# Feed-forward products of a two-layer trunk: seven half-size products for eight, with h through DRAM

## The chip, the cores and the metric

The kernel runs on one core of a Trainium2 chip. The metric is the time of one execution on the device, in microseconds (us). Before the change three runs took 2847.48, 2851.25 and 2854.4 us; the median is 2851.25.

## What is computed

Two layers, each a token-mixing sublayer and a gated feed-forward, in float32, for 1024 tokens of width 1024:

```python
x = layer_norm(ALPHA * x + mix, ln1_g, ln1_b)
up = causal_dwconv(jnp.einsum('bsd,df->bsf', x, w_up), ffn_conv_w)
a, b = jnp.split(up, 2, axis=-1)
ffn = jnp.einsum('bsf,fd->bsd', jax.nn.silu(a) * b, w_down)
return layer_norm(ALPHA * x + ffn, ln2_g, ln2_b)
```

`w_up` has 2 × 2816 columns and `w_down` 2816 rows. The convolution runs over time, three taps for each channel. `mix` comes from three token mixers (window pooling, banded attention, gated convolution), which the change leaves alone.

## The kernel before

Every float32 product is made of three matmuls of float32r operands: high × high, high × low, low × high. `split` makes the two parts: ACT casts to float32r (L94), and DVE or POOL subtracts that from the source (L98). `product` issues the three matmuls (L114 to L116); each has 128 rows of the contraction, 128 stationary columns and 512 moving ones. The contraction of the up-projection has 8 tiles of 128 (k), its columns go by 22 tiles of 128 (f) for a and 22 for b.

PE and SP (the queue that issues loads) execute in the order in which the program is written; ACT, DVE and POOL are ordered by a scheduler that knows priorities (`urgent`, `high_priority`). Tiles come from rings: "ws" (3 buffers) for weights as loaded, "wh" and "wl" (3 each) for their parts, "T" (30) and others; a buffer is written anew only when its last readers are done. PSUM has three "mm" tiles of two banks and two "ax" tiles of one bank.

- `weight`: SP loads [128, 1024] of a weight (L106), ACT casts it, POOL subtracts.
- `up`: a column tile's product with x over both halves of the tokens goes into one mm tile (`half`, `column`), then `then`: ACT multiplies by the last tap (L710), DVE adds the other two (L713, twice). When both columns of f are there, ACT applies silu (L716), DVE multiplies (L717), and the result h is split into high and low parts that stay in SBUF.
- `down`: for two f at a time (four at the end), the products of all 8 token tiles with the two rows of `w_down`, added to the residual y by DVE (L773, L775). These products are written between columns of the next two f, so that PE has work at any time. In the last group each token tile is normalised (`norm`) as soon as it is done, and `to_features` transposes it on PE (L313) and splits it for the next layer.
- `feed_forward` begins with `lead`: the first halves of three columns, between which the token tiles that still come from `output` are transposed.
- `output` is the last product of the mixer: its result is added to x (L691), normalised, and given to `to_features` piece by piece (`pending`).
- `norm`: DVE takes statistics (L272) and scales (L281), then some operations on one element a partition, then ACT (L303) and POOL or DVE (L304).

## Time and profile before

| | |
|---|---|
| median of three runs | 2851.25 us |
| profiled execution: span | 2849.9 us |
| PE busy | 2805.1 us, 98%, 12388 matmuls and transposes |
| DVE busy | 1179.7 us, 41% |
| ACT busy | 834.3 us, 29% |
| POOL busy | 819.2 us, 29% |
| DMA | 169.73 MB, mean 60 GB/s |

The span is the time of one profiled execution, from its first to its last instruction. Busy times are sums over instructions of an engine; matmuls are pipelined, so the shown length of one is longer than the time by which the next follows. A row of a group of instructions has the line, the engine, the operation, output <- inputs, the shape and the count, then busy us and the mean ns of one, then the idle time of the engine just ahead of them with what ended it.

### The profile page before, as it was taken

Reading aid. Unit: us, or ns where it says so; the run is one execution under the profiler, and the core shown is the slowest. Engines: PE = TensorE matmul, PEld = TensorE weight load, DVE = VectorE, ACT = ScalarE, POOL = GpSimd, SP = SyncE. Lnnn points to the kernel's source line nnn. Section 1 sums busy time; section 2 is a strip of 40 time slices with the busy share of each in tenths; the row PEclk is TensorE's granted clock in tenths of the full one; section 3 lists DMA queues with packets and bytes.
Section 4 is the critical chain, followed back from the end, with each engine's and each line's share of the span. In section 5 each row is a group of like instructions: output and inputs, shape, how many; then the busy total and the mean of one; then the engine's idle time right before and its main releaser. Section 6 shows DMA issues by size and latency. Waiting matters only on the chain. (4 is left out here: it accounts for less than half of the span.)

```text
span 2849.9 us, 29730 instructions
## 1 busy us (share of the span) xinstructions
PE 2805.1 (98%) x12388; PEld 2295.4 (81%) x12388; DVE 1179.7 (41%) x1567; ACT 834.3 (29%) x1218; POOL 819.2 (29%) x363
## 2 busy tenths in 40 slices
PE   9999999999999999999999999999999999999998
PEld 7777888887888888888777778888878888888886
DVE  5576011137334333333756761011363443333337
ACT  4446112124322222222334461121343222222222
POOL 2222233345222222222322223333452222222223
PEclk9999999999999999999999999999999999999999
DMA  4101111142111111111230011111421111111111
GB/s 158 38 31 37 45 45 52 52 148 96 52 45 52 45 45 52 52 52 45 82 105 25 30 37 52 45 52 45 155 89 52 52 45 45 49 56 52 45 52 74
DMA packets 48966, 169.73 MB, mean 60 GB/s; under 512 B 6720, under 2 KB 7616, under 8 KB 48832
## 3 DMA queue, kind: packets, MB, share of 16 engines
q1 hardware_dynamic: 46656, 164.54, 16.3%
q10 hardware_dynamic: 2176, 3.30, 0.5%
q8 instruction: 97, 1.59, 0.2%
q14 instruction: 37, 0.30, 0.0%
HBM read 156.97 MB, written 9.54 MB: 58 GB/s over the span
## 5 line engine op out<-in xcount | busy, mean ns | idle before, releaser
L114 PE MATMUL mm<-T,wh 128*128 128x512 f32 x2880 | 1133.7, 394 | 1.5 <-ACT T L94 1.4
L115 PE MATMUL mm<-T,wh 128*128 128x512 f32 x2880 | 1126.5, 391 | 0.8 <-DVE T L98 0.8
L116 PE MATMUL mm<-T,wl 128*128 128x512 f32 x2880 | 1125.9, 391 | 0.0
L98 POOL TENSOR_TENSOR wl<-ws,wh 128x1024 fp32r<-128x1024 f32 (+2 forms) x264 | 632.8, 2404 | 1709.8 <-ACT wh L94 1641.3
L114 PEld LDWEIGHTS mm<-T,wh 128*128 128x128 f32 x2880 | 543.3, 189 | 116.9 <-ACT T L94 2.7
L116 PEld LDWEIGHTS mm<-T,wl 128*128 128x128 f32 x2880 | 543.2, 189 | 113.8 <-POOL wl L98 0.4
L115 PEld LDWEIGHTS mm<-T,wh 128*128 128x128 f32 x2880 | 543.4, 189 | 112.5 <-DVE T L98 1.9
L94 ACT CAST wh<-ws 128x1024 fp32r<-128x1024 f32 (+1 forms) x265 | 272.3, 1036 | 1103.7 <-PE mm L115 509.6
L713 DVE SCALAR_TENSOR_TENSOR t<-mm,par,t 128x1023 f32<-128x1023 f32 (+1 forms) x176 | 225.7, 1282 | 677.4 <-ACT t L710 675.0
L548 DVE TENSOR_TENSOR t<-t,mm 128x1024 f32<-128x1024 f32 x48 | 58.6, 1221 | 465.6 <-PE mm L116 465.6
L775 DVE TENSOR_TENSOR T<-T,mm 128x1024 f32<-128x1024 f32 x143 | 174.3, 1219 | 111.1 <-PE mm L116 111.1
L114 PE MATMUL mm<-wh,T 128*128 128x512 f32 x318 | 124.2, 390 | 0.0
L116 PE MATMUL mm<-wh,pt 128*128 128x512 f32 x318 | 123.9, 390 | 0.0
L114 PE MATMUL mm<-wh,s 128*128 128x512 f32 x318 | 123.9, 390 | 0.0
L115 PE MATMUL mm<-wl,T 128*128 128x512 f32 x318 | 123.9, 390 | 0.0
L116 PE MATMUL mm<-wh,T 128*128 128x512 f32 x318 | 123.8, 389 | 0.0
L115 PE MATMUL mm<-wl,s 128*128 128x512 f32 x318 | 123.8, 389 | 0.0
L685 PE MATMUL mm<-wl,T 128*128 128x512 f32 x256 | 101.5, 396 | 1.4 <-POOL wl L98 1.4
L684 PE MATMUL mm<-wh,T 128*128 128x512 f32 x256 | 101.6, 397 | 0.0
L686 PE MATMUL mm<-wh,T 128*128 128x512 f32 x256 | 100.3, 392 | 0.0
L710 ACT ACTIVATE t<-mm,par 128x1024 f32<-128x1024 f32 x88 | 97.3, 1106 | 5.2 <-PE mm L116 5.2
L98 POOL TENSOR_TENSOR ql<-T,q 64x512 fp32r<-64x512 f32 x32 | 44.0, 1374 | 168.6 <-DVE q L96 128.6
(180 smaller groups left out, 2383.2 us busy)
## 6 DMA issues: line engine op xcount, KB each, us to landing
ws<-in_w_up SPq DMA_DIRECT2D x88, 512.0 KB
ws<-in_w_in SPq DMA_DIRECT2D x75, 512.0 KB
ws<-in_w_down SPq DMA_DIRECT2D x44, 512.0 KB
ws<-in_w_o SPq DMA_DIRECT2D x40, 512.0 KB
ws<-in_w_ac SPq DMA_DIRECT2D x8, 512.0 KB
ws<-in_w_b SPq DMA_DIRECT2D x8, 512.0 KB
T<-in_x SPq DMA_DIRECT2D x8, 512.0 KB
T<-in_ln SPq DMA_DIRECT2D x8, 512.0 KB
```

The costliest lines, as they stand in the source:

```text
L94: self.nc.scalar.copy(hi, src)
L98: return eng.tensor_tensor(lo, src, hi.bitcast(F32), op=ALU.subtract)
L114: self.nc.tensor.matmul(out, wh, xh, start=start and i == 0, stop=False)
L115: self.nc.tensor.matmul(out, wh, xl, start=False, stop=False)
L116: self.nc.tensor.matmul(out, wl, xh, start=False, stop=stop and i == n - 1)
L548: return st["sig"], self.nc.vector.tensor_tensor(st["sig"][:], st["sig"][:], pb[:], op=ALU.mult)
L684: nc.tensor.matmul(out, hi[:, k, ts], wh[:, es], start=first, stop=False)
L685: nc.tensor.matmul(out, hi[:, k, ts], wl[:, es], start=False, stop=False)
L686: nc.tensor.matmul(out, lo[:, k, ts], wh[:, es], start=False, stop=end)
L710: nc.scalar.mul(y[:], ps[:], w(2))
L713: nc.vector.scalar_tensor_tensor(y[:, d:], ps[:, :S - d], w(k), y[:, d:], op0=ALU.mult, op1=ALU.add)
L775: nc.vector.tensor_tensor(y[:], y[:], ps[:], op=ALU.add)
```

## The change

Both products of the feed-forward are cut in two along each side, and the four blocks are multiplied with seven products in place of eight (Strassen's scheme in Winograd's form). Sums and differences of blocks are made ahead of a product on its operands, and behind it on its results.

*Up.* For each f, with a11 and a12 the two halves (in k) of column tile f, a21 and a22 those of f + 22, and B11, B12, B21, B22 the blocks of x (halves in k, halves of tokens), the seven products P1 to P7 go to the halves of two mm tiles, ab and cd. Each has 4 k tiles × 3 = 12 matmuls. `begin` has P1 and P2, `rest` P3 to P7. ACT copies P1, u2 and u3 out of PSUM, DVE adds them to later products. The combinations of x (T1 to T4) are made by `to_combined` when token tiles 4 to 7 arrive; x's operands now take 28 of the "T" buffers, and "wh" and "wl" become one ring "w" of 6. The combinations of the weights are made on POOL in each step. The results c go on from SBUF (`activated`); L numbers of the listings are those of the changed kernel.

*h.* It is no longer split in SBUF. For every two f POOL makes S1 to S4 from h, and ACT's queue writes seven blocks to DRAM.

*Down.* It runs behind all steps of `up`, one product ("run") after another: A11, A12, S2, S1, S3 for all four pairs of token tiles q, then S4 and A22 for q = 0, 1 and again for q = 2, 3. Each run goes over 11 blocks j of 2 × 128 rows; the operands of each j are loaded (h block and `w_down`), combined (S2, A22) and split. The residual y goes through DRAM (`spill1`) too.

```diff
-    BUFS = {"T": 30, "t": 4, "s": 3, "pt": 3, "q": 1, "ql": 1, "ws": 3, "wh": 3, "wl": 3}
+    BUFS = {"T": 30, "t": 4, "s": 3, "pt": 3, "q": 1, "ql": 1, "ws": 3, "w": 6}
...
+    def made(self, src, e_lo="vector"):
+        t = self.new([P, 2, HALF], F32R, "w")
+        self.split(t[:, 0, :], t[:, 1, :], src, "scalar", e_lo)
+        return t[:, 0, :], t[:, 1, :]
+
     def up(self, l, f):
...
+        def run(ps, a, b, fresh, end):
+            wh, wl = a
+            self.product(ps, [(wh[:, k * P:(k + 1) * P], wl[:, k * P:(k + 1) * P],
+                               self.xc[b][0][k // 2][:, k % 2, :], self.xc[b][1][k // 2][:, k % 2, :])
+                              for k in range(4)], fresh, end, True)
+
+        def begin():
+            a11, a12 = st["a1"] = load(0)
+            w11, w12 = self.made(a11, "gpsimd"), self.made(a12)
+            ab = st["ab"] = self.mm()
+            run(ab[:, lo], w11, "B11", True, False)
+            st["u"] = self.new([P, 2, HALF], F32, "s")
+            p1 = st["u"][:, 0, :]
+            nc.scalar.copy(p1, ab[:, lo])
+            run(ab[:, hi], w12, "B21", True, True)
+            st["c"] = [self.new([P, S], F32, "t") for _ in range(2)]
+            nc.vector.tensor_tensor(st["c"][0][:, lo], p1, ab[:, hi], op=ALU.add)
+
+        def rest():
...
+            nc.gpsimd.tensor_tensor(s1[:], a21, a22, op=ALU.add)
+            sub(a21, a11, a21)
+            sub(a11, s1[:], a11)
+            w2 = self.made(a11)
+            w1 = self.made(s1[:])
+            w3 = self.made(a21)
+            w22 = self.made(a22)
+            sub(a12, a12, a11)
+            w4 = self.made(a12)
+            cd = self.mm()
+            run(ab[:, lo], w2, "T2", False, False)
+            u2 = st["u"][:, 1, :]
+            nc.scalar.copy(u2, ab[:, lo])
+            run(cd[:, lo], w1, "T1", True, False)
+            run(ab[:, lo], w3, "T3", False, True)
+            u3 = self.new([P, HALF], F32, "s")
+            with self.urgent():
+                nc.scalar.copy(u3[:], ab[:, lo])
+                nc.vector.tensor_tensor(cb[:, hi], u3[:], cd[:, lo], op=ALU.add)
+            run(cd[:, hi], w22, "T4", True, True)
+            nc.vector.tensor_tensor(cb[:, lo], u3[:], cd[:, hi], op=ALU.subtract)
+            run(cd[:, lo], w4, "B22", False, True)
+            nc.vector.tensor_tensor(ca[:, hi], u2, cd[:, lo], op=ALU.add)
+            self.activated(l, f, ca, cb)
...
+        nc.gpsimd.tensor_tensor(s1, a21, a22, op=ALU.add)
+        nc.gpsimd.tensor_tensor(s3, a11, a21, op=ALU.subtract)
+        nc.gpsimd.tensor_tensor(s2, s1, a11, op=ALU.subtract)
+        nc.gpsimd.tensor_tensor(s4, a12, s2, op=ALU.subtract)
+        for name, src in (("A11", a11), ("A12", a12), ("A22", a22), ("S1", s1), ("S3", s3), ("S2", s2), ("S4", s4)):
+            nc.scalar.dma_start(four(self.hs[STATIONARY.index(name), f // 2]), src)
...
+            elif name == "S2":
+                b1 = self.new([P, 1024], F32, "ws")
+                nc.sync.dma_start(b1[:], w0)
+                nc.sync.dma_start(st[:, hi], w1[:, hi])
+                k = kept[j] = self.new([P, 2, HALF], F32, "T")
+                t2[j] = self.new([P, 2, HALF], F32, "T") if j % 2 == 0 else t2[j - 1]
+                other = t2[j][:, j % 2, :]
+                nc.gpsimd.tensor_tensor(k[:, 0, :], b1[:, hi], b1[:, lo], op=ALU.subtract)
+                nc.gpsimd.tensor_tensor(other, st[:, hi], k[:, 0, :], op=ALU.subtract)
+                nc.gpsimd.tensor_tensor(k[:, 1, :], st[:, hi], b1[:, hi], op=ALU.subtract)
...
+        runs = [(n, range(4)) for n in range(5)] + [(n, qs) for qs in ((0, 1), (2, 3)) for n in (5, 6)]
+        for n, qs in runs:
...
+            for j in range(NJ):
+                wh, wl = operands(name, j, qs)
+                for q in qs:
+                    ts = slice(q * P, (q + 1) * P)
+                    self.product(banks[q], [(wh[:, ts], wl[:, ts], wh[:, hi], wl[:, hi])], fresh and j == 0, closes and j == NJ - 1, True)
+                if n == 0 and j == 4:
+                    for t in range(8):
+                        y[t] = self.new([P, D], F32, "T")
+                        nc.sync.dma_start(y[t][:], self.spill1[t])
...
     def to_combined(self, y, t):
...
+            nc.vector.tensor_tensor(t1, b12[:], b11, op=ALU.subtract)
+            nc.vector.tensor_tensor(t3, f22, b12[:], op=ALU.subtract)
+            nc.vector.tensor_tensor(t2, f22, t1, op=ALU.subtract)
+            parts("B22", f22, "gpsimd")
+            parts("T2", t2, "vector")
+            parts("T1", t1, "vector")
+            nc.gpsimd.tensor_tensor(t2, t2, b21, op=ALU.subtract)
+            parts("T3", t3, "vector")
+            parts("T4", t2, "gpsimd")
 
     def feed_forward(self, l):
...
+        for f in range(2):
+            self.pending(1 - f)
+            ups[f][0]()
+            self.pending(1 + f)
+        self.pending(len(self.pend))
+        for f in range(NFF):
+            if f > 1:
+                ups[f][0]()
+            ups[f][1]()
+        self.down(l)
```

The order of instructions, with the waits for other engines' semaphores. PE, up-projection of layer 0, before: the end of a column's first half and the start of its second, both in one mm tile.

```order
L114 MATMUL mm_6711<-T_3983,wh_6706 128x512
L115 MATMUL mm_6711<-T_3984,wh_6706 128x512
L116 MATMUL mm_6711<-T_3983,wl_6707 128x512
L114 MATMUL mm_6711<-T_4341,wh_6706 128x512
L115 MATMUL mm_6711<-T_4342,wh_6706 128x512
L116 MATMUL mm_6711<-T_4341,wl_6707 128x512
```

PE after: the end of P1 and the start of P2, both in one mm tile (ab).

```order
L117 MATMUL mm_7396<-T_3979,w_7390 128x512
L118 MATMUL mm_7396<-T_3981,w_7390 128x512
L119 MATMUL mm_7396<-T_3979,w_7390 128x512
L117 MATMUL mm_7396<-T_3982,w_7393 128x512 [waits Activation_49]
L118 MATMUL mm_7396<-T_3984,w_7393 128x512
L119 MATMUL mm_7396<-T_3982,w_7393 128x512
```

The first matmul of P2 has gained a wait for ACT, which is the copy of P1 (L737).

ACT, up-projection of layer 0, before: casts of loaded weights, multiplications by a tap, silu.

```order
L710 ACTIVATE t_7876<-mm_7827,par_280 128x1024 [waits PE_49]
L716 ACTIVATE t_7876<-t_7876 128x1024 [waits DVE_49,Activation_49]
L94 CAST wh_8070<-ws_8069 128x1024 [waits DMAHW2_49,PE_49,Pool_49]
L710 ACTIVATE t_7935<-mm_7886,par_280 128x1024 [waits PE_49]
L94 CAST s_7941<-t_7876 128x1024 [waits DVE_49]
L94 CAST wh_8129<-ws_8128 128x1024 [waits DMAHW3_49,PE_49,Pool_49]
```

ACT after, the stretch from the copy of P1 to that of P3, u2 (L737 P1, L761 u2, L790 silu, L807 writes of h, the T tiles being S1 to S4):

```order
L737 COPY s_6411<-mm_6398 128x512 [waits PE_49]
L97 CAST w_6447<-ws_6390 128x512 [waits Activation_49]
L790 ACTIVATE pt_6367<-pt_6367 128x1024 [waits DVE_49,Activation_49]
L97 CAST w_6529<-ws_6527 128x512 [waits DMAHW0_49,PE_49]
L807 DMA h_blocks_4802<-pt_6367 512x1x128 [waits DVE_49]
L807 DMA h_blocks_4802<-pt_6367 512x1x128
L807 DMA h_blocks_4802<-T_6377 128x512 [waits Pool_49]
L807 DMA h_blocks_4802<-T_6378 128x512 [waits Pool_49]
L807 DMA h_blocks_4802<-T_6378 128x512 [waits DMAHW1_49,Pool_49]
L761 COPY s_6411<-mm_6398 128x512 [waits PE_49]
L97 CAST w_6532<-ws_6527 128x512
L97 CAST w_6571<-ws_6527 128x512 [waits PE_49]
```

Five writes of h now stand between the silu and the copy u2, three of them with a wait for POOL.

POOL after, in the same stretch (L749 and L745 are combinations of weights, L101 is a split, L802 to L805 make S1 to S4); before, POOL had one split of 128x1024 for each weight.

```order
L803 TENSOR_TENSOR T_6377<-pt_6230 128x512 [waits DMAHW4_49]
L749 TENSOR_TENSOR ql_6567<-ws_6565 128x512 [waits DMAHW3_49,DVE_49]
L745 TENSOR_TENSOR ws_6565<-ws_6527,ws_6565 128x512 [waits DMAHW0_49,DVE_49,Pool_49]
L101 TENSOR_TENSOR w_6529<-ws_6527,w_6529 128x512 [waits Activation_49]
L745 TENSOR_TENSOR ws_6527<-ql_6567,ws_6527 128x512 [waits Pool_49]
L802 TENSOR_TENSOR T_6377<-pt_6230,pt_6367 128x512 [waits DVE_49]
L804 TENSOR_TENSOR T_6378<-T_6377,pt_6230 128x512 [waits DMAHW6_49,DMAHW5_49,Pool_49]
L805 TENSOR_TENSOR T_6378<-pt_6367,T_6378 128x512 [waits Pool_49]
L745 TENSOR_TENSOR ws_6527<-ws_6527 128x512 [waits DVE_49]
```

S1, S2 and S4 (L802, L804, L805) follow four operations on weights, of which the first waits for a load.

SP, down-projection of layer 0, before: loads of `w_down` between loads of `w_up`.

```order
L106 DMA ws_6457<-in_w_down 128x1024 [waits DMAHW5_49,Pool_49]
L106 DMA ws_6463<-in_w_down 128x1024 [waits DMAHW6_49,Pool_49]
L106 DMA ws_6581<-in_w_up 128x1024 [waits DMAHW7_49,Pool_49]
L106 DMA ws_6640<-in_w_up 128x1024 [waits DMAHW0_49,Pool_49]
L106 DMA ws_6705<-in_w_up 128x1024 [waits DMAHW1_49,Pool_49]
L106 DMA ws_6764<-in_w_up 128x1024 [waits DMAHW2_49,Pool_49]
```

SP after, the run S2: the h block (L828), the whole row block of `w_down` (L838) and half of the next (L839) for each j.

```order
L828 DMA ws_8559<-h_blocks_4802 128x512 [waits DMAHW6_49,DMAHW5_49,DVE_49]
L838 DMA ws_8563<-in_w_down 128x1024 [waits DMAHW7_49,DMAHW0_49,DVE_49]
L839 DMA ws_8559<-in_w_down 128x512
L828 DMA ws_8587<-h_blocks_4802 128x512 [waits DMAHW2_49,DMAHW1_49,DVE_49]
L838 DMA ws_8591<-in_w_down 128x1024 [waits DMAHW3_49,DMAHW5_49,DVE_49,Pool_49]
L839 DMA ws_8587<-in_w_down 128x512
L828 DMA ws_8614<-h_blocks_4802 128x512 [waits DMAHW4_49]
L838 DMA ws_8618<-in_w_down 128x1024 [waits DMAHW0_49,DMAHW6_49,DVE_49,Pool_49]
```

The load at L838 waits for POOL from the second j on; that is the third combination (L845) of the j ahead, which reads the slot.

271 lines of the change are left out of this document (166 added, 105 removed).

## Prediction

> **What bounds the kernel now.** I read the page's first part, then the windows by stage, then groups of instructions, then the timeline at places where engines hand over. The page:
>
> ```profile
> span 2849.9 us, 29730 instructions
> PE 2805.1 (98%) x12388; PEld 2295.4 (81%) x12388; DVE 1179.7 (41%) x1567; ACT 834.3 (29%) x1218; POOL 819.2 (29%) x363
> L116 PE MATMUL mm<-T,wl 128*128 128x512 f32 x2880 | 1125.9, 391 | 0.0
> ```
>
> PE is busy for 98% of the span: the kernel is bound by the number of its matmuls. One is shown as 391 ns long, but they overlap; their spacing comes from the windows in the middle of the feed-forward (us, then PE, PEld, DVE, ACT and POOL busy with counts, PEclk, DMA share, GB/s), with two windows at the borders of layers and phases behind them:
>
> ```profile
> 1000.00:1300.00 300.00, 300.00 (x1325) 248.59 (x1324) 108.58 (x89) 68.22 (x66) 68.51 (x29) 1.00 0.14 50
> 2400.00:2700.00 300.00, 300.00 (x1325) 248.50 (x1324) 114.84 (x94) 65.08 (x63) 66.97 (x28) 1.00 0.14 48
> 1404.00:1436.00 32.00, 26.43 (x131) 21.29 (x130) 30.72 (x64) 14.67 (x32) 14.94 (x6) 0.96 0.20 83
> 2100.00:2116.00 16.00, 13.19 (x60) 10.11 (x60) 15.06 (x22) 7.68 (x10) 12.68 (x6) 1.00 0.49 164
> ```
>
> In both feed-forward windows PE is busy 300 of 300 us with 1325 matmuls: 300/1325 = 0.2265 us each. The clock is 1.00, and DVE, ACT and POOL are idle for more than half. PE loses time only at borders: 32 − 26.43 = 5.6 us at the layer's end, 16 − 13.19 = 2.8 us where the feed-forward of layer 1 starts.
>
> **The matmuls removed.** Before, a layer's up-projection takes 44 columns × 2 halves × 8 k tiles × 3 = 2112 matmuls of 128x512, its down-projection 22 × 8 × 2 × 3 = 1056. After, it is 22 × 7 × 12 = 1848 and 11 × 7 × 12 = 924. Gone are 264 and 132 a layer, at 0.2265 us 59.8 and 29.9 us, for two layers 179.4 us. This is certain. A product of 12 matmuls lasts 2.72 us, a step f has 7 of them: 19.0 us, where two columns took 96 × 0.2265 = 21.7.
>
> **The up-projection: four waits in each step.** The order shows that the first matmuls of P2, P3, P6 and P7 wait for an ACT copy or a DVE add that reads what the product just ahead has written, in the same mm tile or the bank to be reused. Nothing else is queued on PE meanwhile. Before, the second half of a tile started with no wait. The hand-over is seen in the attention:
>
> ```profile
> 1593.24 1.28 DVE L98 TENSOR_TENSOR pt<-ax,pt 128x512 fp32r<-128x512 f32 x2
> 1593.98 1.97 PE L456 MATMUL ax<-pt,T 128*128 128x512 f32 x4 [2.57 <-DVE pt L98]
> 1595.99 0.58 ACT L460 COPY T<-ax 64x512 f32<-64x512 f32 x1 [2.51 <-PE ax L456]
> 1596.60 0.69 DVE L461 TENSOR_TENSOR T<-T,ax 64x512 f32<-64x512 f32 x1 [1.29 <-ACT T L460]
> ```
>
> ACT starts 0.04 us after the shown end of the matmuls (1593.98 + 1.97), DVE 0.03 after ACT, and PE 0.06 after the first of the two DVE splits (1593.24 + 0.69). The shown end is 391 − 226 = 165 ns behind the time at which the next matmul could go. The operations themselves, 128x512 out of PSUM:
>
> ```profile
> L94 ACT CAST pt<-ax 128x512 fp32r<-128x512 f32 x60 | 32.4, 589 | 58.6 <-PE ax L443 58.5
> L98 DVE TENSOR_TENSOR pt<-ax,pt 128x512 fp32r<-128x512 f32 x60 | 38.8, 685 | 26.8 <-ACT pt L94 26.3
> ```
>
> A wait on a copy costs 0.165 + 0.03 + 0.59 + 0.06 = 0.84 us (P1 to P2), on an add 0.165 + 0.04 + 0.685 + 0.06 = 0.95 (P2 to P3, P6 to P7), on a copy and an add 1.56 (P5 to P6): together 4.30 us. P5 waits for u2, which P4 covers. A step becomes 19.03 + 4.30 = 23.3 us, longer than the 21.7 it replaces. 22 of them cost 94.6 us a layer. At the least the engines start at once, so 4.2; late engines add up to 0.7 (DVE has two adds, four shifted multiply-adds, a product and five or six splits in a step, 2 × 0.69 + 4 × 1.28 + 1.25 + 5.5 × 0.69 = 11.5 us), so 92 to 110; I take 94.6:
>
> ```profile
> L713 DVE SCALAR_TENSOR_TENSOR t<-mm,par,t 128x1023 f32<-128x1023 f32 x88 | 113.0, 1284 | 675.0 <-ACT t L710 675.0
> L710 ACT ACTIVATE t<-mm,par 128x1024 f32<-128x1024 f32 x88 | 97.3, 1106 | 5.2 <-PE mm L116 5.2
> L717 DVE TENSOR_TENSOR t<-t,t 128x1024 f32<-128x1024 f32 x44 | 55.0, 1250 | 0.9
> L716 ACT ACTIVATE t<-t 128x1024 f32<-128x1024 f32 x44 | 46.7, 1061 | 114.1 <-DVE t L713 114.1
> ```
>
> **The h writes stand in ACT's queue.** Every second step the order has on ACT five DMA writes of h blocks, and behind them the copy u2 on which P5 waits. The last wait for POOL's S1, S2, S4, and POOL has four operations of the next weights ahead of these, which need a weight load whose slot comes free only with the split of w22. POOL's rows:
>
> ```profile
> L98 POOL TENSOR_TENSOR wl<-ws,wh 128x1024 fp32r<-128x1024 f32 x259 | 627.5, 2430 | 1666.2 <-ACT wh L94 1605.8 <-PE ax L456 52.3 <-issue 3.5
> L98 POOL TENSOR_TENSOR ql<-T,q 64x512 fp32r<-64x512 f32 x32 | 44.0, 1374 | 168.6 <-DVE q L96 128.6 <-DVE m L422 20.2 <-DVE den L432 19.3
> L98 POOL TENSOR_TENSOR wl<-ws,wh 128x128 fp32r<-128x128 f32 x4 | 3.5, 882 | 37.8 <-ACT wh L94 29.6 <-ACT t L509 8.1
> ```
>
> 128x512 on POOL lies between half of 2430 (1.22) and a line from the 128- to the 1024-wide row (1.55); nearest is the 64x512 row, 1.37. A load:
>
> ```profile
> GB/s 0 0 297 266 389 348 10 0 0 0 0 0 0 0 0 92 276 420 369 144 10 0 0 0 0 0 0 0 0 164 256 420 328 348 420 379 338 277 307 317
> L106 SPq DMA_DIRECT2D ws<-in_w_o x2: 328/328/328, 2045.3 to 2050.7; - x2
> ```
>
> In slices of 0.4 us, the load issued at 2045.3 moves data until about 2048; issue and landing take 2.7 to 3 us. Counted from P7's start in the step before: split of w22 at about 5, load landed at 8.1, seven POOL operations 9.6, then the issue and the copy: u2 at about 18.7. P5 is due at 5 × 2.72 + 0.84 + 0.95 = 15.4. PE stalls 3.2 (POOL at 1.3) to 5.5 us (at 1.55, a late split); I take 4.3, in 11 pairs 47 a layer (35 to 60). Up per layer: −59.8 + 94.6 + 47 = **+82** (67 to 110).
>
> **The down-projection, seven runs over 11 blocks j** (12 matmuls, 2.72 us each).
> *Start*: A11 reads the h blocks just written, and y is loaded in the middle of it (8 × 512 KB); the last pair's writes are late by the chain above. Between 0, if loads run ahead, and 12 us; taken 10.
> *S2*: each j needs two of the three ws slots; the load of b1 for j+1 waits for POOL's third combination of j (L845 in the order). So load (3.0) and three POOL operations (4.1) go one after another: 7.1 us against 2.72. With 1.5 j loaded ahead: 9.5 × 7.1 + 5 = 73 against 29.9, +43 (30 to 55).
> *S4 and A22*, by pairs of q: 6 matmuls, 1.36 us a j. A slot is held for the load, two casts and two splits, about 5 us, over three slots 1.7 a j; for A22 POOL's combination adds 1.4: 2.1. Four runs take 2 × 18.7 + 2 × 23.5 = 84, against 60. The norms of two tiles stand on DVE between the operands of one run and the next:
>
> ```profile
> L272 DVE BATCH_NORM_STATS2 st<-T 128x6 f32<-128x512 f32 x64 | 42.0, 681 | 0.2
> L281 DVE SCALAR_TENSOR_TENSOR T<-T,mv,T 128x1024 f32<-128x1024 f32 x32 | 56.0, 1751 | 0.4
> L304 DVE TENSOR_TENSOR T<-T,T 128x1024 f32<-128x1024 f32 x8 | 9.6, 1222 | 2.7 <-ACT T L303 2.7
> L98 DVE TENSOR_TENSOR T<-ax,T 128x256 fp32r<-128x256 f32 x104 | 41.0, 419 | 59.7 <-ACT T L94 59.0
> L94 ACT CAST T<-ax 128x256 fp32r<-128x256 f32 x104 | 36.4, 371 | 54.5 <-PE ax L313 40.4 <-DVE T L98 12.4 <-issue 0.7
> ```
>
> A norm is 2 × 0.68 + 1.75 + 1.22 and small ones, about 5 us; two are 10, of which three blocks made ahead (4 us) cover a part: some 3 us at each of four ends. Together +34 (10 to 45); the border S3 to S4 +2.
> Down per layer: −29.9 + 10 + 43 + 34 + 2 = **+59** (35 to 85).
>
> **Start and end of the phase.** Before, the first halves of three columns (3 × 24 matmuls, 16.3 us) cover the last norms and transposes, and 2.8 us are lost. After, only two `begin`s (4 products, 10.9 us) go ahead, since P3 needs T2 of all tiles. DVE has, from the last product of the output on: four adds (4 × 0.685, as a copy's split), two norms (10), and for four tiles three combinations each (12 × 0.685) and six splits (24 × 0.42), with four weight splits 34 us together; ahead of P3 stand the 10.9 and two transposes of 1 us. The gap is 34 − 13 = 21 us, less the 2.8: some **+20** a layer (8, if two of the tiles are done beside the output's last products, to 30). At the end of the layer and the tail I take **+3** (0 to 6): the norms follow the last product as before.
>
> **Sum.** 82 + 59 + 20 + 3 = 164 a layer, 328 for two. The profiled execution's 2849.9 becomes 3178; it lies 1.35 us below the median of the runs, 2851.25, which is within their spread (2847.48 to 2854.4), so I forecast 3178 us. Of this change 0.2% (some 6 us) could be told from nothing.
>
> **Rivals.**
> *PE stays the bound (faster).* If ACT and DVE release the mm tile within the time of a matmul and all loads run ahead, the matmuls alone count: 2849.9 − 179.4 + 2 × 3 = 2676 us. For it speaks how idle ACT and DVE are; against it the waits in the order, whose operations cannot start before the product has ended. The point of decision is 179.4/44 = 4.08 us lost per step f, all losses counted; the four waits alone are 4.30. Chance 0.03.
> *Only the four waits and the starts bite*: the loads run ahead in the down-projection and POOL is never late. 2849.9 − 179.4 + 189.2 + 40 + 6 = 2906; with S2's serial loads, whose slots the order fixes, 2992. Chance 0.14.
> *DVE and POOL slow each other, and the stalls grow.* After gives POOL 4 to 6 operations in each step beside DVE's. A row where both work:
>
> ```profile
> L98 DVE TENSOR_TENSOR T<-T,T 128x512 fp32r<-128x512 f32 x8 | 9.0, 1150 | 18.1 <-ACT T L94 18.1
> ```
>
> This 128x512 split between SBUF tiles takes 1150 where others take 685. If a third of DVE's 11.5 us and POOL's 9.6 are longer by that ratio, 1.68, the chain to u2 grows by 2.2 us in 11 pairs and S2's by 0.9 in 11 j, and the adds after products by 0.2 a wait: 24 + 10 + 18 = 52 a layer, 3282. The Trainium skill, GPSIMD Engine Reference, section 8, Key points, says that GpSimd shares its SBUF interfaces with VectorE, with contention for DVE instructions of two SBUF inputs; the row of 1150 agrees, the 685 of splits out of PSUM too. Chance 0.15.
> *The clock falls in the stalls.* The windows, PEclk third from the end:
>
> ```profile
> 656.00:660.00 4.00, 1.31 (x8) 1.13 (x9) 2.03 (x5) 2.06 (x6) 4.00 (x2) 0.86 0.00 0
> 660.00:664.00 4.00, 4.00 (x15) 3.23 (x15) 1.18 (x3) 1.96 (x4) 1.40 (x2) 0.72 0.00 0
> 2112.00:2116.00 4.00, 1.81 (x13) 1.51 (x13) 3.10 (x5) 4.00 (x5) 0.97 (x1) 1.00 0.41 131
> ```
>
> With 1.31 of 4 us busy the clock fell to 0.86, and to 0.72 in the next 4; with 1.81 busy it stayed at 1.00. If each of the 22 stalls ahead of P5 and four stalls at starts and borders costs as the first did, 4 × (0.14 × 0.33 + 0.28) = 1.3 us, 34 us come on top, 3212; if products in S2 and S4 also run at 0.72, those not hidden by loads (60 × 2 us × 0.39) 47 more, 3259. The Trainium skill, TensorE: Matmul & The Clock Gate, Part 1, has the clock halved after at least one idle window of about 3.4 us; by that each such stall would cost about 1.7 us, an estimate from that page, 44 for 26. The trace shows both outcomes, so 0.08.
> My forecast keeps 0.60. The range of 80% reaches from 3030, which takes in the second rival's upper case with late starts, to 3320, the third rival with its bounds. Slower by over 0.2%: 0.96, same 0.01, faster 0.03.
>
> **What would show it.** In the profile after: PE's busy share falls to about 83% (matmul time 2805 − 179 = 2626 of 3178). P2, P3, P6 and P7 idle ahead of their first matmul 0.8, 0.95, 1.5 and 0.95 us with ACT or DVE as releaser; P5 idles some 4 us every second f, released by ACT's u2. S2's run lasts about 73 us with POOL over half busy; S4 and A22 together about 94; PE has a gap of about 20 us at the start of each feed-forward. I am wrong if step f lasts 20 us or less, if the writes of h do not hold up u2, or if S2 keeps near 2.72 us a j.

## The result, and the profile after

The changed kernel takes 3340.8 us (median of 4 runs, 3338.71 to 3346.45), the kernel before 2852.82 (4 runs): a ratio of 1.1716, 95% interval 1.1699 to 1.1733. The forecast was 3178 us with a range to 3320. Slower is right, and so are most of the places; the size is 163 us short, and the time is 21 us above the range.

The page of the changed kernel:

```profile
span 3344.7 us, 31427 instructions
PE 2843.8 (85%) x11596; PEld 2212.6 (66%) x11596; DVE 1575.7 (47%) x2270; ACT 1146.2 (34%) x1907; POOL 1109.7 (33%) x675
L117 PE MATMUL mm<-T,w 128*128 128x512 f32 x2704 | 1114.4, 412 | 272.5 <-ACT s L761 81.3
L117 PE MATMUL mm<-w 128*128 128x512 f32 x484 | 215.2, 445 | 127.0 <-ACT w L97 126.8
L761 ACT COPY s<-mm 128x512 f32<-128x512 f32 x44 | 25.8, 585 | 242.4 <-POOL T L805 177.2
```

PE has 792 matmuls and transposes fewer, and its busy time is nevertheless longer than before (2805.1). A group that took 391 ns a matmul takes 412 to 445: the matmuls themselves became slower. The third row has PE's idle time ahead of first matmuls of products; 81.3 us of it ended with the copy u2 (L761), which itself waited 177.2 us for POOL's S4 (L805).

Windows of the changed kernel (us, PE, PEld, DVE, ACT and POOL busy, PEclk, DMA share, GB/s): the middle of the up-projection, the start of the feed-forward in layer 0, the run of S2 in layer 0, the four runs of S4 and A22 in layer 1:

```profile
1000.00:1300.00 300.00, 235.62 (x909) 176.30 (x908) 140.64 (x163) 97.49 (x142) 115.27 (x78) 0.93 0.23 74
690.00:782.00 92.00, 61.71 (x224) 45.48 (x223) 68.79 (x99) 40.40 (x81) 44.80 (x36) 0.81 0.16 57
1400.00:1483.00 83.00, 53.41 (x137) 35.37 (x136) 24.76 (x32) 13.53 (x24) 38.23 (x31) 0.73 0.40 136
3190.00:3331.00 141.00, 79.60 (x267) 55.08 (x265) 90.42 (x157) 50.88 (x97) 30.71 (x22) 0.77 0.42 134
```

Where 1325 matmuls stood in 300 us there are 909, and PEclk, 1.00 in the middle of both feed-forwards before, is 0.93, 0.81, 0.73 and 0.77. The waits of PE in the first of these windows (us in total, times, longest):

```profile
PE mm L117 <- ACT s L761: 24.4, 6, 4.1
PE mm L117 <- DVE t L767: 15.4, 11, 1.4
PE mm L117 <- DVE t L769: 8.6, 11, 0.8
PE mm L117 <- DVE t L740: 8.6, 11, 0.8
PE mm L117 <- ACT s L737: 7.4, 11, 0.7
```

The lower four are the four waits of each of 11 steps: 0.7, 0.8, 1.4 and 0.8 us. With the 0.165 us by which a matmul is shown too long they are 0.83, 0.94, 1.56 and 0.94, in sum 4.27; the forecast was 4.30. The first is the wait for u2, in every second step, 4.07. From the timeline, P2 to P5 of such a step (start, us, operation, and in brackets the idle time ahead with its releaser):

```profile
1110.28 2.98 SPq L721 DMA_DIRECT2D ws<-in_w_up  x2
...
1111.65 0.50 PE L117 MATMUL mm<-T,w 128*128 128x512 f32 x1 [0.68 <-ACT s L737]
...
1111.99 0.39 PE L118 MATMUL mm<-T,w 128*128 128x512 f32 x1
...
1113.89 1.34 POOL L749 TENSOR_TENSOR ql<-ws 128x512 f32<-128x512 f32 x1 [13.82 <-DMA ws<-in_w_up]
...
1115.32 2.37 POOL L745 TENSOR_TENSOR ws<-ws,ws 128x512 f32<-128x512 f32 x1
...
1117.64 1.29 POOL L101 TENSOR_TENSOR w<-ws,w 128x512 fp32r<-128x512 f32 x1
1119.01 1.29 POOL L745 TENSOR_TENSOR ws<-ql,ws 128x512 f32<-128x512 f32 x1
1120.26 1.28 POOL L802 TENSOR_TENSOR T<-pt,pt 128x512 f32<-128x512 f32 x1
1121.57 3.01 ACTq L807 DMA_DIRECT2D h_blocks<-T  x3
1121.62 1.26 POOL L804 TENSOR_TENSOR T<-T,pt 128x512 f32<-128x512 f32 x1
1122.96 1.26 POOL L805 TENSOR_TENSOR T<-pt,T 128x512 f32<-128x512 f32 x1
1124.62 0.58 ACT L761 COPY s<-mm 128x512 f32<-128x512 f32 x1 [8.86 <-POOL T L805]
...
1125.26 0.80 PE L117 MATMUL mm<-T,w 128*128 128x512 f32 x1 [4.07 <-ACT s L761]
```

The chain is the one forecast: the weight load lands at 1113.9, POOL has its operations on the next weights ahead of S1 to S4, ACT's last write waits for S4, and the copy u2 stands behind that write. PE then starts P5 after 4.07 us of idle time with a matmul of 0.80 us in place of 0.39. The clock has fallen: P5's 12 matmuls span 4.86 us from the first start to the last, where those of an undisturbed product span 2.49. Of the 20 stalls of this kind 18 are followed by 4.86, the other two by 3.95 and 4.22.

The start of the feed-forward in layer 0 (DVE's norm of tile 7, its transposes on PE, the splits of the combinations, and two waits of step 0's P3):

```profile
713.09 1.22 DVE L307 TENSOR_TENSOR t<-t,T 128x1024 f32<-128x1024 f32 x1 [1.22 <-ACT t L306]
...
727.94 1.45 PE L939 MATMUL ax<-ident,t 128*128 128x128 f32 x8 [0.68 <-ACT w L955]
...
733.51 6.53 DVE L101 TENSOR_TENSOR T<-w,T 128x256 fp32r<-128x256 f32 x8
...
736.03 0.80 PE L117 MATMUL mm<-T,w 128*128 128x512 f32 x1 [6.64 <-ACT w L97]
741.23 0.80 PE L119 MATMUL mm<-T,w 128*128 128x512 f32 x1 [3.98 <-DVE w L101]
```

From the last matmul of the output product to the first of step 2 it takes 87.1 us in layer 0 and 89.9 in layer 1, for 14 products that need 38.1. This stretch is called the start below. In layer 0 some 11 us of it are matmuls at a fallen clock: step 0's P1, for one, spans 5.37 us in place of 2.49.

A place the forecast does not have, in layer 1 behind S4's first run:

```profile
3217.48 1.48 SPq L920 DMA_DIRECT2D out<-T  x2
3219.07 0.40 SPq L828 DMA_DIRECT2D ws<-h_blocks  x1
...
3225.20 0.79 PE L117 MATMUL mm<-w 128*128 128x512 f32 x1 [15.51 <-ACT w L97]
```

SP issues in the order of the program. Its stores of finished tiles (L920) wait for their norms until 3217.48, the loads for the next run stand behind them, and PE idles for 15.5 us; there are three such gaps (15.5, 17.1 and 16.6 us).

Stage by stage the trace gives the following, against the matmuls' own time at 0.2265 us each (both layers, in us; the forecast's terms are those of the prediction, its start already less what the kernel before lost there):

| term | forecast | measured |
|---|---|---|
| matmuls gone | −179 | −179 |
| four waits × 44 steps | 189 | 188 (4.27 each) |
| first matmuls of products slower | 0 | 26 (0.60 a step) |
| stall ahead of P5 | 94 (22) | 85 (20 × 4.23) |
| clock behind that stall | 0 | 49 (mostly 2.55 each) |
| start of the feed-forward, without its waits | 40 | 81 (39.2 + 42.1) |
| A11 | 20 | 28 (43.7 and 44.4 for 29.9) |
| S2 | 86 | 104 (82.3 and 81.5 for 29.9) |
| S4, A22 and their border | 72 | 129 (108 and 140 for 60) |
| remainder: ends of the layers, less what the kernel before lost at these places | 6 | −16 |
| sum | 328 | 495 |

The spans differ by 494.8; the last measured row is what is left to that sum.

### The profile page after: what moved, and what is told of

Read it like the earlier page. It is cut to its first block, busy times and chain, and to the rows that moved or that the text cites. A ratio compares the mean times of both kernels' runs of the same rounds, so it can differ in the third digit from the quotient of the medians.

```text
span 3344.7 us, 31427 instructions
## 1 busy us (share of the span) xinstructions
PE 2843.8 (85%) x11596; PEld 2212.6 (66%) x11596; DVE 1575.7 (47%) x2270; ACT 1146.2 (34%) x1907; POOL 1109.7 (33%) x675
## 4 chain that ended last, share of the span: by engine, by line
PE 65%; DVE 12%; POOL 7%; DMA 7%; ACT 4%; issue 4%; SPq 0%; ACTq 0%; DVEq 0%; POOLq 0%
PE mm L117 20%; PE mm L118 18%; PE mm L119 18%; DMA ws<-in_w_down 4%; DVE w L101 2%; DMA h_blocks<-pt 1%; PE mm L416 1%; PE mm L691 1%; PE mm L690 1%; POOL ws L745 1%; PE mm L692 1%; DVE T L284 1%; PE mm L415 1%; ACT w L97 1%; PE ax L459 1%
## 5 line engine op out<-in xcount | busy, mean ns | idle before, releaser
L117 PE MATMUL mm<-T,w 128*128 128x512 f32 x2704 | 1114.4, 412 | 272.5 <-ACT s L761 81.3
L119 PE MATMUL mm<-T,w 128*128 128x512 f32 x2704 | 1085.2, 401 | 19.5 <-DVE w L101 16.5
L118 PE MATMUL mm<-T,w 128*128 128x512 f32 x2704 | 1084.5, 401 | 1.2 <-DVE T L101 1.2
L117 PEld LDWEIGHTS mm<-T,w 128*128 128x128 f32 x2704 | 524.3, 194 | 468.5 <-DVE t L767 94.5
L97 ACT CAST w<-ws 128x512 fp32r<-128x512 f32 (+2 forms) x687 | 474.1, 700 | 1004.8 <-PE mm L119 409.8
L119 PEld LDWEIGHTS mm<-T,w 128*128 128x128 f32 x2704 | 525.8, 194 | 140.0 <-DVE w L101 18.7
L101 POOL TENSOR_TENSOR w<-ws,w 128x1024 fp32r<-128x1024 f32 (+3 forms) x180 | 382.5, 2127 | 690.3 <-ACT w L97 616.8
L101 DVE TENSOR_TENSOR w<-ws,w 128x512 fp32r<-128x512 f32 (+2 forms) x507 | 378.8, 762 | 479.5 <-ACT w L97 463.3
L118 PEld LDWEIGHTS mm<-T,w 128*128 128x128 f32 x2704 | 526.4, 195 | 105.3 <-DVE T L101 2.1
L117 PE MATMUL mm<-w 128*128 128x512 f32 x484 | 215.2, 445 | 127.0 <-ACT w L97 126.8
L749 POOL TENSOR_TENSOR ql<-ws 128x512 f32<-128x512 f32 x44 | 57.8, 1313 | 605.0 <-DMA ws<-in_w_up 459.3
L118 PE MATMUL mm<-w,w 128*128 128x512 f32 x484 | 217.6, 450 | 39.5 <-DVE w L101 38.9
L119 PE MATMUL mm<-w,w 128*128 128x512 f32 x484 | 208.1, 430 | 0.0
L118 PEld LDWEIGHTS mm<-w,w 128*128 128x128 f32 x484 | 103.5, 214 | 82.4 <-DVE w L101 61.2
L787 DVE SCALAR_TENSOR_TENSOR T<-t,par,T 128x1023 f32<-128x1023 f32 x88 | 113.9, 1294 | 29.2 <-ACT T L784 27.6
L787 DVE SCALAR_TENSOR_TENSOR pt<-t,par,pt 128x1023 f32<-128x1023 f32 x88 | 113.7, 1292 | 27.4 <-ACT pt L784 27.2
L119 PEld LDWEIGHTS mm<-w,w 128*128 128x128 f32 x484 | 104.3, 216 | 21.1
L101 DVE TENSOR_TENSOR w<-T,w 128x512 fp32r<-128x512 f32 x66 | 54.3, 823 | 117.5 <-ACT w L97 117.5
L761 ACT COPY s<-mm 128x512 f32<-128x512 f32 x44 | 25.8, 585 | 242.4 <-POOL T L805 177.2
```

Source lines behind the costliest of these rows:

```text
L97: self.nc.scalar.copy(hi, src)
L101: return eng.tensor_tensor(lo, src, hi.bitcast(F32), op=ALU.subtract)
L117: self.nc.tensor.matmul(out, wh, xh, start=start and i == 0, stop=False, skip_group_check=more)
L118: self.nc.tensor.matmul(out, wh, xl, start=False, stop=False, skip_group_check=more)
L119: self.nc.tensor.matmul(out, wl, xh, start=False, stop=stop and i == n - 1, skip_group_check=more)
L749: nc.gpsimd.tensor_tensor(s1[:], a21, a22, op=ALU.add)
```

## The experiments

They are edits of the changed kernel (3340.8 us), except where another is named. A run is given with its median and its ratio to the kernel before.

**The four waits.** The second halves of ab and cd get one-bank tiles of their own (the idle "ax" ring), so that P2, P3, P6 and P7 do not have to wait for readers of the other half. An added dependency keeps the copy u2 behind POOL's S4, where it stood in the changed kernel by the order of ACT's queue.

```diff
-            ab = st["ab"] = self.mm()
+            a0 = self.mm()
+            st["ab"] = a0[:, lo], (self.aux()[:] if f > 1 else a0[:, hi])
...
-            cd = self.mm()
+            cd_lo, cd_hi = self.mm()[:, lo], self.aux()[:]
...
-            nc.scalar.copy(u2, ab[:, lo])
+            copied = nc.scalar.copy(u2, ab_lo)
+            if f > 1 and f % 2 == 0:
+                self.after(copied, self.s4)
```

> From the third step f on, the second halves of ab and cd are tiles of their own (one bank each), so that PE need not wait at P2, P3, P6 and P7 for the copy or add of the product just ahead; the writes of h stay ahead of the copy u2. My theory (the four waits cost what the profile of the changed kernel shows, 0.83 + 0.94 + 1.56 + 0.94 = 4.27 us and 0.55 us for slower first matmuls, in 40 steps 193 us; the stall ahead of P5 grows by up to 2 us in 20 pairs, since P5 comes due sooner): 3341 - 193 + 40 = 3190 us, between 3150 and 3230. Rival (ACT and DVE need the time anyway, so the step hardly shortens): 3290 or more.

Measured 3193.21 us, 1.1196 (1.1163 to 1.1228): −148. All four are gone in its trace. They were waits for the tile, not for the data: P1 and P2, for one, write the two banks of one tile, and P2 waited for the reader of P1's bank. The Trainium skill, PSUM — Partial Sum Buffer, section "PSUM bank collisions raise a hardware error", asks for PSUM to be guarded by bank. By that rule too a wait for the whole tile of two banks was more than is needed; the run agrees with its 148 us. The wait for u2 then grows from 4.07 to 6.83, since PE arrives earlier at the same chain:

```profile
1029.86 0.80 PE L117 MATMUL mm<-T,w 128*128 128x512 f32 x1 [6.83 <-ACT s L763]
```

**The stall ahead of P5.** The seven writes of h are issued behind the copy u2 of the next step.

```diff
-            nc.scalar.copy(u2, ab[:, lo])
+            copied = nc.scalar.copy(u2, ab[:, lo])
+            while self.writes:
+                self.writes.pop()(copied)
```

> The writes of h are issued behind the copy u2 of the next step; nothing else changes. My theory (P5 waits 4.2 us because u2 stands behind the writes, and its 12 matmuls and the next wait then take 2.6 us more at a fallen clock): 20 pairs x 6.8 us = 137 us gone, 3341 - 137 = 3205 us, between 3190 and 3230, and P5's matmuls follow at 0.2265 us everywhere. Rival A (the clock falls for another reason, such as the mean load of PE): 20 x 4.2 = 84 us gone, 3257 us. Rival B (POOL is late for the weights as well, and the stall moves to the next product): 3300 or more.

Measured 3210.91 us, 1.1258 (1.1225 to 1.1291): −130. Nearly every step lasts 23.90 us now, P5 spans 2.49, and in a window of the up-projection the clock is back although the four waits are all still there:

```profile
1000.00:1100.00 100.00, 84.69 (x352) 64.48 (x351) 59.75 (x64) 37.78 (x54) 44.08 (x31) 1.00 0.26 87
```

So waits of 0.7 to 1.4 us leave the clock alone, and the stall of 4.07 us is what took it.

**S2's slots.** b1 comes from the "t" ring, which is idle in the down-projection, in place of "ws".

```diff
-                b1 = self.new([P, 1024], F32, "ws")
+                b1 = self.new([P, 1024], F32, "t")
```

> The whole row block that the run S2 loads goes to a ring of four buffers that is idle then, in place of the ring of three that the run shares. My theory (S2's 82 us come from load and three POOL operations one after another, because the slot comes free only with the third): the run falls to POOL's pace, 11 x 3 x 1.3 = 43 us, 39 a layer, 3341 - 78 = 3263 us. Rival (S2 is bound by the transfers, 1 MB for each block): 11 blocks at 200 GB/s are 58 us, 24 a layer, 3293 us.

Measured 3276.67 us, 1.1489 (1.1455 to 1.1522): −64, between the 78 of the theory and the 48 of the rival; S2 takes 48.6 us in both layers in place of 82.3 and 81.5. The rest above 29.9 isn't these slots: POOL, which makes the three combinations of each j, is now busy for 45.0 of 49 us.

```profile
1397.00:1446.00 49.00, 36.00 (x135) 24.33 (x134) 34.16 (x32) 12.95 (x23) 45.03 (x30) 1.00 0.57 193
```

**SP's stores.** The stores of finished tiles are issued behind the loads of the next run.

```diff
-            nc.sync.dma_start(self.out[t], y[:])
+            self.stores.append(lambda: nc.sync.dma_start(self.out[t], y[:]))
```

> In the last layer the stores of the output stand on SP's queue behind the loads of the next run, in place of ahead of them. My theory (layer 1's S4 and A22 take 140 us against 108 in layer 0 because SP waits for a norm ahead of a store, and the next run's loads stand behind it): 32 us gone, less some 3 for stores at the very end, 3312 us. Rival (the norms hold DVE, whichever queue the stores are in): no more than 8 us gone, 3333 us or more.

Measured 3314.28 us, 1.162 (1.1587 to 1.1654): −27; layer 1's four runs of S4 and A22 ("the four runs" below) take 111 us in place of 140, about what layer 0's take.

**These four together.**

> The edits of the four kernels before together. Alone they took 148, 130, 64 and 27 us off 3341. My theory (the four losses lie at different places and add up; the stall ahead of P5, which grew when the four waits went, is gone too, some 2 to 3 us in 20 pairs more): 3341 - 369 - 50 = 2922 us, between 2895 and 2975. Rival (with PE faster, DVE, ACT or POOL become the bound in the step, which then takes more than its 19.0 us of matmuls): a step of 21 us, 2922 + 40 x 2 = 3002 us or more.

Measured 2928.66 us, 1.0259 (1.0241 to 1.0276): −412. Steps of 19.04 and 20.2 us, where 7 products are 19.03:

```profile
1000.00:1100.00 100.00, 97.91 (x431) 80.29 (x430) 73.68 (x76) 44.80 (x65) 53.90 (x37) 1.00 0.31 98
```

The four edits alone sum to 148 + 130 + 64 + 27 = 369. Together they are worth 43 more. The likely reason is the first one's: alone, it lets the stall ahead of P5 grow by 2.76 us in 20 steps, 55 us, which the second takes away.

**The start: three edits that hardly move it.** The low parts of T1 to T4 are not made (fewer splits on DVE, and T4's on POOL):

```diff
-            parts("T2", t2, "vector")
-            parts("T1", t1, "vector")
+            half("T2", t2)
+            half("T1", t1)
```

> The changed kernel without the low parts of the four combinations of x (T1 to T4): their splits are left out at the start of the phase, and P3 to P6 use the high part in place of the low one, so the count of matmuls is the same. My theory (the 40 us lost at the start of each feed-forward are the work of DVE, whose 24 splits of 128x256 there take 0.77 us on the mean, 18 us): 18 us a layer gone, 3305 us, between 3290 and 3318. Rival (norms and transposes one behind another, with the fallen clock, set that gap): 8 us a layer or less, 3325 us or more.

Measured 3327.62 us, 1.1665 (1.164 to 1.1689); the starts take 79.9 and 82.9 us, −7 each. My theory that DVE's splits alone set the start fell. Next, the norms of tiles 6 and 7 left out:

```diff
-                            self.norm(zs[4 * h + t], g, b, "vector" if h else "gpsimd")
+                            if 4 * h + t < 6:
+                                self.norm(zs[4 * h + t], g, b, "vector" if h else "gpsimd")
```

> The changed kernel without the first norm of token tiles 6 and 7 (they go on unnormalised). Asks what sets the 40 us lost at the start of each feed-forward. Theory A (a chain: add, norm, transposes, combinations of the last tiles, one behind another): the two norms' 20 us between the last product of the output and the transposes of tile 7 shrink to some 5 us, 13 to 15 us a layer gone, 3312 us, between 3305 and 3320. Theory B (DVE and POOL slow each other, so that the sum of DVE's work counts): two norms of 5 us are 10 a layer, 3321 us, the next kernel tells more.

Measured 3332.28 us, 1.1687 (1.1666 to 1.1709), slower than either theory said; starts 83.4 and 81.2, −4 and −9. And POOL's share of the combinations given to DVE, so that the two don't work side by side there:

```diff
-            parts("B22", f22, "gpsimd")
+            parts("B22", f22, "vector")
...
-            nc.gpsimd.tensor_tensor(t2, t2, b21, op=ALU.subtract)
+            nc.vector.tensor_tensor(t2, t2, b21, op=ALU.subtract)
```

> The changed kernel with the low parts of B22 and T4 and the last difference for T4 made by DVE in place of POOL, so that POOL has only the weights' work at the start. Theory A (a chain of the last tiles): DVE gets 4 tiles x (4 x 0.42 + 0.69) = 9.5 us more, of which the tiles ahead of the last hide a half; 5 us a layer slower, 3351 us. Theory B (DVE's 24 splits at 0.77 in place of 0.42 us are slowed by POOL beside them, 8 us, and the differences too): DVE's extra work is paid back, 3341 us or down to 3330.

Measured 3344.26 us, 1.1729 (1.1708 to 1.1751): no change clear of noise; starts 88.9 and 93.0. The trace tells more than the time:

```profile
L101 DVE TENSOR_TENSOR T<-w,T 128x256 fp32r<-128x256 f32 x80 | 32.0, 446 | 2.4 <-ACT T L97 2.4
```

With no part of the combinations on POOL beside it, a split of DVE's takes 446 ns; in the changed kernel the same operation takes 766 (its row is shown further below). So DVE makes 80 splits in 32.0 us where it made 48 in 34.7. The slowing by POOL is real, and its removal pays for the work that DVE takes over, but not for more.

**The start: the combinations left out.** T1 to T4 and B22 of tiles 4 to 7 aren't made:

```diff
-            self.xc[b] = tile4(), tile4()
+            self.xc[b] = self.xc["B11" if b in ("T2", "T1") else "B21"]
```

> The changed kernel with one part of the computation left out: the combinations T1 to T4 and B22 of tiles 4 to 7 and their splits aren't made, and the products P3 to P7 of every step take B11 and B21 in their place (same matmuls, same waits of the steps). It asks what sets the start of the feed-forward, where the changed kernel takes 87.1 and 89.9 us from the last output matmul to step 2 for 38.1 us of matmuls, of which the waits of two steps are 9.6. Theory A (the combinations and their splits, started late because the transposes stand behind step 1's first products on TensorE, hold P3 of step 0): both starts fall by 25 us or more, to 50 to 62; 3341 - 2 x 30 = 3281 us (3263 to 3291). Theory B (the norms ahead and the fallen clock, each engine a little): no more than 10 us of each, 3321 us or above.

Measured 3284.09 us, 1.1501 (1.1484 to 1.1519): −57. The starts take 59.9 and 59.8 us, −27 and −30; of the 39 and 42 us beyond products and step waits about 12 are left.

The norms of tiles 4 to 7 are left out on top:

```diff
-                            self.norm(zs[4 * h + t], g, b, "vector" if h else "gpsimd")
+                            if not h:
+                                self.norm(zs[t], g, b, "gpsimd")
```

> As the kernel without combinations, and the norms of tiles 4 to 7 after the output product are left out too (their residual sums go on unnormalised). Theory A: little is left for the norms, 5 us of each start at most below the kernel without combinations (3271 to 3281 us). Theory B: it is these norms that hold the first products' weights, so that the starts fall only here, by 25 us or more each, to 50 to 62 us, and the time to about 3275 us from 3321 or above.

Measured 3281.87 us, 1.1505 (1.149 to 1.1521); starts 56.3 and 59.1: the norms were no more than 4 us of it. So it is the combinations and their splits that hold the start, as a whole. Taking a part of them away, or to another engine, gives little; probably because the rest still runs through ACT, DVE and POOL in turn, which no run shows by itself.

**Easing the down-projection ("the eased kernel").** The four together, plus: one of S2's combinations on DVE, more slots and priority for the operands of S4 and A22, y loaded tile by tile.

```diff
-            st = self.new([P, 1024], F32, "ws")
+            st = self.new([P, 1024], F32, "ws" if len(qs) == 4 or j % 2 else "t")
...
-                nc.gpsimd.tensor_tensor(k[:, 1, :], st[:, hi], b1[:, hi], op=ALU.subtract)
+                nc.vector.tensor_tensor(k[:, 1, :], st[:, hi], b1[:, hi], op=ALU.subtract)
...
+                with self.urgent() if len(qs) == 2 else ExitStack():
```

> The four edits, and in the down-projection: one of S2's three combinations on DVE in place of POOL, operands of S4 and A22 through seven slots in place of three with their splits ahead of the norms, and y loaded tile by tile in place of all at once. My theory (S2 stands at POOL's pace of 4.4 us a block, S4 and A22 at their three slots and the norms, A11 at y's loads): S2 from 48.6 to 34, S4 and A22 from 108 to 75, A11 from 44 to 38, 53 a layer: 2922 - 106 = 2816 us, between 2780 and 2870. Rival (S4 and A22 wait for the norms themselves or the transfers): only S2's 14 a layer, 2890 us or more.

Measured 2871.68 us, 1.0067 (1.0052 to 1.0082): −57 to the four together, and 56 above the 2816 expected, just outside the range. A11 takes 37.2 and 35.4, S2 42.3 and 43.9, the four runs 92 and 98. Windows of these runs in both layers:

```profile
1334.00:1428.00 94.00, 72.59 (x305) 56.17 (x303) 92.72 (x158) 53.29 (x113) 39.57 (x25) 0.93 0.60 195
2755.00:2853.00 98.00, 73.00 (x265) 54.30 (x264) 89.69 (x155) 47.16 (x97) 33.21 (x22) 0.86 0.52 171
```

In layer 0 DVE is busy for 92.7 of 94 us and sets the time, in layer 1 for 89.7 of 98. Some of this is waiting for POOL: of its 42 splits of 128x512 in layer 0's window the 30 without POOL at work beside them take 0.68 us, the 10 with POOL at work for most of their time 1.67 on the mean. S2 is the clearer case. With one combination moved to DVE it was to fall to 34 us, and DVE is now busy for 41.3 of 42, its splits at 1.23 and 1.04 us in place of 0.68:

```profile
1232.00:1274.00 42.00, 34.33 (x132) 26.39 (x132) 41.32 (x41) 13.39 (x23) 29.77 (x19) 0.92 0.65 221
L101 DVE TENSOR_TENSOR w<-ws,w 128x512 fp32r<-128x512 f32 x12 | 14.7, 1226 | 0.7 <-ACT w L97 0.7
L101 DVE TENSOR_TENSOR w<-T,w 128x512 fp32r<-128x512 f32 x12 | 12.4, 1039 | 0.0
```

In every second step P7 also waits up to 1.2 us for DVE's u3 sum.

**Three more attempts on that kernel, all misses.** All h writes behind u3, stores and transposes later:

```diff
-            while self.writes:
-                self.writes.pop()(copied)
...
-                nc.scalar.copy(u3[:], ab_lo)
+                copied = nc.scalar.copy(u3[:], ab_lo)
...
+            while self.writes:
+                self.writes.pop()(copied)
```

> The kernel of e7 with three more edits: the writes of h go behind the copy u3 as well (in e7 P7 waits 1.2 us in every second step, since u3 stands behind a write that waits for POOL), the last layer's stores go out in the middle of the run after the next (in e7 9 us of PE are lost where loads stand behind them), and the transposes for the next layer are placed later in S4 (9 us lost in layer 0, where PE comes to a transpose before its norm is done). My theory: 20 x 1.2 + 9 + 9 = 42 us gone, 2872 - 42 = 2830 us, between 2815 and 2850, faster than the kernel before. Rival (the casts that now follow the writes come too late for their products, or the norms only wait elsewhere): 2860 us or more.

Measured 2938.32 us, 1.0303 (1.0288 to 1.0317). The writes now stand ahead of the next step's copy of P1, on which P3 waits, and the wait comes back there, some 2.7 us on the mean, every second step:

```profile
1033.51 0.50 PE L117 MATMUL mm<-T,w 128*128 128x512 f32 x1 [2.65 <-ACT s L739]
```

Only the last two writes behind u3:

```diff
+            if self.writes:
+                self.writes[0](copied, slice(0, 5))
...
+            if self.writes:
+                self.writes.pop()(copied, slice(5, 7))
```

> The kernel of e7 with one edit: only the writes of S2 and S4 go behind the copy u3, the other five stay behind u2, where e8 moved all seven. My theory (in e7 P7 waits 1.2 us in every second step because u3 stands behind the write of S2, which waits for POOL; e8 lost more than that, since all seven writes then stood ahead of the casts for P3): 20 x 1.2 = 24 us gone, 2872 - 24 = 2848 us, between 2840 and 2860. Rival (as in e8, the casts behind the two writes are late for their products): 2870 us or more.

Measured 2890.06 us, 1.0128 (1.0111 to 1.0145). P7's wait is 1.7 us and not gone: on ACT a cast and the five other writes stand ahead of u3, and S1's write waits for POOL.

The same, with the last addition of the final norms on POOL:

```diff
-            self.norm(y, g, b, "vector")
+            self.norm(y, g, b, "gpsimd")
```

> e11, and the last addition of the norms behind the down-projection made by POOL in place of DVE. Theory (S4 and A22 are bound by DVE, which has 12 us of splits, 10 of norms and some 4 of additions and transposed splits for a run of 15 us; an addition of 1.2 us per tile leaves it): 8 tiles x 1.2 us in layer 0, as many in layer 1, 10 to 20 us gone, 2833 us, between 2825 and 2845. Rival (POOL's 2.4 us in place of 1.2, in the chain of a norm, and its hold on DVE beside it cost as much): 2848 us or more.

Measured 2900.31 us, 1.0166 (1.0151 to 1.0181); the four runs of layer 0 take 101 us.

**The end without norms.** The eased kernel, with the norms at the end of both layers left out.

```diff
-            self.norm(y, g, b, "vector")
```

> The eased kernel (2871.68 us) with the norms at the end of both layers left out: the sums of the down-projection go on and out unnormalised. In the eased kernel the four runs of S4 and A22 take 92 and 98 us for 60 of matmuls. Theory (VectorE is short there: with eight norms beside the splits it is the latest of the chain): the runs fall to 60 to 72 us in both layers, and the border and the tail by 4 each; 2872 - 22 - 28 - 8 = 2814 us (2805 to 2830). Rival (GpSimd's A22 combination, or the loads): no more than 8 us of each layer, 2850 us or above.

Measured 2830.27 us, 0.992 (0.9906 to 0.9933): −41, just outside what was expected. The four runs take 84 and 79 us, −8 and −19, and not 60 to 72. The norms are a part; without them DVE is still busy for 75 of 84:

```profile
1335.00:1419.00 84.00, 71.26 (x297) 54.01 (x296) 75.23 (x112) 44.93 (x102) 35.00 (x24) 0.96 0.63 195
```

**The transposes earlier.** The eased kernel, the transposes of tiles 6 and 7 ahead of and in between step 1's first products.

```diff
+            if f == 1:
+                self.pending()
             run(ab_hi, w12, "B21", True, True)
...
-            self.pending(1 + f)
+            self.pending(2)
```

> The eased kernel (2871.68 us) with all of the computation; only the place of two groups of transposes on TensorE is another. The transposes of tile 6 stand ahead of step 1's first product and those of tile 7 between its first and its second; in the eased kernel both stand behind both products, at 724.6 and 726.3 us, where tile 7's norm ends at 712.9. Theory A (the combinations hold P3): they start about 10 us earlier, and each start falls by 8 to 10 us: 2872 - 18 = 2854 us (2848 to 2862), the time of the kernel before. Theory B (the sum of VectorE's and ScalarE's work in the start decides, wherever the transposes stand): step 1's weights come later by what the combinations come earlier, and the time is 2866 to 2878 us.

Measured 2871.57 us, 1.0063 (1.005 to 1.0075): nothing. The wait moved from step 0's P3 to step 1's P1, whose weights' cast stands behind the combinations' casts on ACT:

```profile
723.02 0.79 PE L117 MATMUL mm<-T,w 128*128 128x512 f32 x1 [6.71 <-ACT w L97]
```

## Why the prediction was short

Slower was forecast and is right. Of the 167 us by which the difference of the spans was short, S4 and A22 are 57, the clock behind the stall 49, the start 41, the first matmuls 26, S2 18 and A11 8; 32 go the other way (the stall itself, the four waits, and the remainder).

**Right.** The 179 us of matmuls; the four waits (188 for 189, and the experiment on halves); the h writes in ACT's queue and the chain through POOL that sets u2 (4.23 us for 4.3); S2's three slots (−64 us when b1 moved). PE's busy share, 85%, is near the 83% forecast, but by luck: the span is longer than forecast, and the matmuls in it got longer too.

**A step that failed: each stall was priced at its length.** The prediction took 4.3 us for the stall ahead of P5 and left the clock to a rival with a chance of 0.08 at 1.3 us a stall. The runs show 4.23 us of stall and mostly 2.55 us behind it: 49 us in 20 stalls. The rival was right in its mechanism and half in its size. The Trainium skill, TensorE: Matmul & The Clock Gate, Part 1, has the clock halved after an idle window of about 3.4 us and given back after a busy one; the estimate from that page was 1.7 us a stall. The trace agrees that stalls of 4.07 us cost the clock every time and waits of 1.4 never did, and measures 2.5 us where the estimate has 1.7. Half of the waits of 1.95 to 3.22 us cost it too (last section), though they are shorter than that window.

**A product's first matmul.** Priced as one of many; behind a wait it is shown at 0.50 us, not 0.39. A step loses 0.60 us beyond its waits, 26 us in all.

**The start.** The step "the gap is 34 − 13 = 21 us" failed in its 34, where it took 419 ns for a split of 128x256. In the changed kernel the splits of the combinations have this group:

```profile
L101 DVE TENSOR_TENSOR T<-w,T 128x256 fp32r<-128x256 f32 x48 | 34.7, 766 | 0.0
```

For 24 of them that is 8 us a layer more. It is POOL's work beside them that makes the difference, since they take 446 ns without it. The step also left out the clock, some 11 us of the 39 in layer 0, and counted DVE alone, while each combination goes through ACT, DVE and POOL, and the casts of step 0's and step 1's weights stand behind them on ACT. Leaving the combinations out gives back 27 and 30 of 39 and 42 us. How these divide between the engines stays open: single parts gave 7, 4 to 9, and nothing.

**S4 and A22, the largest miss.** "1.7 and 2.1 a j", from slots, with 3 us for norms at each end, gave a loss of 72 us for both layers with the border; the trace has 129. The stores in SP's queue, which the prediction does not name, cost 27 us in layer 1. The slots were a limit, as forecast: seven of them with priority took 15 and 14 us off the four runs. Behind them stands DVE's total, busy 92.7 of 94 us in the eased kernel's layer 0; the prediction counted what DVE has at the ends of runs, not over the whole run. Without the norms the runs still take 24 and 20 us more than their 60; what holds these is not shown.

**S2 and A11.** S2's serial chain was right, 82 for 73 us; A11 took 14 us above its matmuls for 10, and 5 to 7 in the eased kernel, where y is loaded tile by tile.

**The rival that DVE and POOL slow each other** (3282) is right in its mechanism: the splits take 766 ns with POOL's part of the combinations and 446 without, and POOL's L745 takes 2.37 us beside DVE in the timeline above, where the 24 of its 132 operations that have no DVE work beside them take 1.26 to 1.29. Its price came from a row that was misread: the 1150 ns are the mean of six splits of 0.68 to 0.69 us and two of 2.54, and these two have POOL at work beside them. So a split is not 1.68 times as long, but either undisturbed or held up for much of a POOL operation. How much of the 488 us is owed to it was not measured apart; moving POOL's part of the start to DVE left the time as it was.

**The prediction's sums.** 84 − 60 + 4 × 3 is 36, taken as 34; 21 − 2.8 is 18, taken as 20; and the lower end of "down", 35, is above the sum of its terms' lower ends, 12. None of these matters to the result.

The losses sum to some 667 us, the 488 and the 179 saved. Four causes are shown by being taken away together: 412. What the scheme saves in matmuls, 179 us, is still not won back in the best complete version here (the eased kernel and the one with earlier transposes, both 0.6 to 0.7% slower than before): the eased kernel keeps 42 and 43 us at the starts, 12 to 14 in S2, 32 to 38 in S4 and A22, 5 to 7 in A11, and 1.0 to 1.5 in every second step. No complete version was faster than the kernel before.

## What to carry to other kernels

Where PE is the bound and every other engine is half idle, count for a scheme that saves matmuls how many new hand-overs it makes for each product, and give each its own PSUM tile, so that a reader of one half does not hold the writer of the other. Look for anything that waits on a slow engine in an in-order queue (an h write on ACT, a store on SP): what stands behind it pays, and if PE stalls for 3.5 us or more, the fallen clock has to be added to the stall. For a short stage, sum each engine's work over that stage; a mean over the kernel (DVE 47%) hides a stage in which it is busy for 99%. And when work is moved between DVE and POOL, look at the mean time of the operations on both: those that run side by side get longer.
